# A hybrid attention encoder on one core: attention A's heads in one written sequence, branch B's results stored by token, and the first tiles scaled straight from PSUM

## The chip, the core and the metric

One core of a Trainium2 chip runs the kernel alone. Its engines have instruction queues of their own and wait for each other by semaphores: PE (TensorE, matrix products into PSUM banks), PEld (its weight loads), DVE (VectorE), ACT (ScalarE), POOL (GpSimd) and SP (SyncE, which here only issues DMA transfers). The metric is the device time of one execution in microseconds; the figure compared is the median of several runs.

## The reference

An encoder layer in float32 over 1280 tokens of 1024 channels: a sample sequence of 1024 and a prompt of 256, each attended within itself. Cut to what matters here:

```
h = rmsnorm(x, g_mix);  z = h @ w_in      # q, k, v of both branches, and two gates
o_a = banded(qa, ka, va, window 128, bias, sink)          # 8 heads, 2 kv heads
for (window, dil) in ((128, 1), (512, 4), (2048, 16)):    # 3 groups of 4 heads
    outs, lses += banded(residues(q, dil), residues(k, dil), residues(v, dil), ...)
alpha = softmax(stack(lses), axis=0);  o_b = sum(alpha * stack(outs))
merged = gate0 * (o_a @ w_branch_a) + gate1 * (o_b @ w_branch_b)
x = x + merged @ w_out
y = rmsnorm(x + relu(rmsnorm(x, g_mlp) @ w_up)**2 @ w_down, g_final)
```

`banded` is softmax attention over a query's own block of keys and the two beside it, with a table of relative biases.

## The kernel before

The tokens are ten tiles of 128 (eight of the sample, `t` 0 to 7, two of the prompt, 8 and 9). Every operand of a large product is split into a high and a low part (`hhi`, `hlo`; ACT makes the high part, DVE the rest), and a product is three matmuls: hi·lo, lo·hi, hi·hi.

**Start.** The weights of the first norm come as one row (`gm_row`); two matmuls with a row of ones (L802) spread it over the partitions into two PSUM banks, and DVE copies each half into `gm` (L803). `square(t)` sums a tile's squares on ACT and takes the root, `scale(t)` multiplies tile, reciprocal root and `gm` on DVE (L707, L708), 16 transposes on PE turn the first two tiles (L340), ACT and DVE split them (L734, L736), and the matmuls of v begin (L764) when ACT has split the first weights `vhi` (L184).

**Projections and branch B** follow in one long part with an order written by hand (`manual_schedule`). Beside its products run, as generators of small steps, branch B's attention (`att_b`), which stores each tile's result to DRAM (`scr_b`, one tensor per group; rows of 132 numbers: the outputs of two heads, their maxima and sums), and `entering()`, which prepares the next part: a raw weight load (`fetch`), queries, keys and values of the first heads (`load_unit(0)`), the biases, and half of h (`h21`, 2 MB), which had been put away in `scr_h`.

**Attention A** (from L1041). 40 steps: four units `u` of two heads, ten tiles each. A step is `scores` (four matmuls into `sc` banks, L1068 and L1069; DVE adds the bias and takes maxima, L1070 and L1074; ACT the exponentials, L1076), then `transposes` (4 or 6 on PE, L1091, copied out of the `pt` banks by DVE and ACT in turn through `copy`, L266 and L268), then `values_of` (the value matmuls, L1106, the copy of `o` and its store by POOL). The three belong to steps i, i − 1 and i − 2 of one pass. Two generators fill in: `logits()`, the gates' products (L191; blocks 0, 2 and 1 of 512, 256 and 512 tokens for each chunk of 128 columns; block 1 needs `h21`), and `merges_of`, which brings branch B's rows back (`load_rows`, six or eight DMAs on SP for two tiles) and merges the three groups by their log sums (DVE, L1158 to L1178). Up to step 36 the tile scheduler may reorder what each engine does; from there the written order holds.

**After it**: `turn_merged` and `turn_a` transpose both results, then come the branch products, gates, `w_out`, the MLP and the last norm.

Of the kernel before, what the change touches and what calls it, by code (L numbers as in the profile page):

```python
# [96 lines left out]
def encoder_kernel(  # L97
# [89 lines left out]
    def mm3(ps, pairs):  # L187

        seq = [x for (lh, ll), (rh, rl) in pairs for x in ((ll, rh), (lh, rl), (lh, rh))]
        for i, (a, b) in enumerate(seq):  # L190
            nc.tensor.matmul(ps, a, b, start=i == 0, stop=i == len(seq) - 1)  # L191
            if i % 8 == 7:
                yield
# [45 lines left out]
    def weight(ahead=None):  # L239
# [4 lines left out]
        while len(raws) < min(len(PLAIN), len(ready) + 1):  # L244
            fetch()
# [28 lines left out]
    scr_b = [dram.tile([T, 2, ROW], F32, name=f"scr_b{g}_") for g in range(3)]  # L274
# [218 lines left out]
    def attention_b(make):  # L493
# [134 lines left out]
    def entering():  # L628
# [33 lines left out]
    with ExitStack() as pre:  # L662
# [137 lines left out]
        for h in range(2):  # L800
            ps = bank("mm", "g")
            nc.tensor.matmul(ps, ones, gm_row[:, 512 * h : 512 * h + 512], start=True, stop=True)  # L802
            nc.vector.tensor_copy(gm[:, 512 * h : 512 * h + 512], ps)  # L803
        square(0)
        scale(0)
        next(turns[0])
        square(1)
        scale(1)
# [6 lines left out]
        split_v(0, 2)  # L815
        scale(2)
# [62 lines left out]
    if True:  # L879
# [159 lines left out]
        flush(True)  # L1039
    first_part.close()  # L1040
# [4 lines left out]
    if True:  # L1045
# [13 lines left out]
        def scores(u, t):  # L1059
# [4 lines left out]
            nm, l = nm_a[:, 2 * u : 2 * u + 2, t], l_a[:, 2 * u : 2 * u + 2, t]  # L1064
# [9 lines left out]
            nc.vector.scalar_tensor_tensor(nm, m, -1.0, nsink[:, 2 * u : 2 * u + 2], op0=ALU.mult, op1=ALU.min)  # L1074
            for h in range(2):
# [3 lines left out]
            live[u, t] = s  # L1079

        def transposes(u, t):
# [14 lines left out]
        def values_of(u, t):  # L1096
            lo, W, _ = tiles[t]
            pt = live.pop((u, t))
            v, rest = units[u][0]["v"]
            pv = bank("pv")  # L1100
            for h in range(2):
                for b in range(W // P):
                    k = lo + b
                    src = v[:, k, HALVES[u // 2]] if k < 8 else rest[:, k - 8, HALVES[u // 2]]
                    for rows_ in HALVES:
                        nc.tensor.matmul(pv[rows_, HD * h : HD * h + HD], pt[:, 2 * b + h, rows_], src,  # L1106
                                         start=b == 0, stop=b == W // P - 1)
# [12 lines left out]
        def logits():  # L1120

            for c in PLAIN:
                hi, lo = weight()
                for t0, n in BLOCKS[::2] + BLOCKS[1:2]:
                    ps = bank("mm")
                    yield from mm3(ps[:, :n], [((hi[:, k, :], lo[:, k, :]), h_at(k, t0, n)) for k in range(KC)])
                    z = wslot("gs", (P, 512))
                    copy(z[:, :n], ps[:, :n])
                    nc.sync.dma_start(scr_g[c][:, t0 : t0 + n], z[:, :n])

        def load_rows(i, t):
# [3 lines left out]
            r = rows_b[i, t] = wslot("r", (P, 2, 3, ROW))  # L1135
            for j in range(2):
                if t < 8:
                    a = P // 8 * (t + j)
                    nc.sync.dma_start(r[:, j, 0, :], scr_b[0][P * (t + j) : P * (t + j + 1), i, :].rearrange(
                        "(q m) c -> m q c", m=8))  # L1140
                    rows = scr_b[1][:NS, i, :].rearrange("(r q m) c -> m r q c", r=4, m=2)[:, :, a : a + 16]
                    for m in range(2):
                        nc.sync.dma_start(r[64 * m : 64 * m + 64, j, 1, :], rows[m])
                    nc.sync.dma_start(r[:, j, 2, :], scr_b[2][:NS, i, :].rearrange(
                        "(r q) c -> r q c", r=8)[:, a : a + 16])
                    continue
                nc.sync.dma_start(r[:, j, 0, :], scr_b[0][P * (t + j) : P * (t + j + 1), i, :].rearrange(
                    "(q m) c -> m q c", m=2))
                for g in (1, 2):
                    nc.sync.dma_start(r[:, j, g, :], scr_b[g][NS:, i, :].rearrange(  # L1150
                        "(r q) c -> r q c", r=2)[:, 64 * j : 64 * j + 64])

        def merge(i, t):

            r = rows_b.pop((i, t))
# [4 lines left out]
            e = small.tile([P, 2, 3, 2], F32, name="e", tag="e", bufs=2)  # L1160
# [747 lines left out]
```

## Time and profile before

| | us |
|---|---|
| median of 3 runs | 1709.33 (1706.9 to 1710.93) |
| the profiled execution, its own time | 1707.63 |
| its span in the profile | 1705.7 |
| attention A, first gate matmul of the stage to the first branch products | about 541 to 711 |

A row of a timeline is: start and duration in us, engine, line of the kernel, operation, out<-in by the program's names, shapes, count, and in brackets how long the engine sat idle before and what ended that. A row of waits is: engine, its operation and line, what it waited for; us in all, times, longest. A row of windows is: the stretch, its length, then for PE, PEld, DVE, ACT and POOL the busy time and in brackets the instructions, then the granted TensorE clock (1.00 is full), the busy share of the DMA engines and GB/s. A row of groups ends with busy us and mean ns of one, then the idle time ahead of the group and what ended it. A row of the chain is start, length and what. Matmuls are pipelined: the distance of two starts is what one costs, its printed duration is longer.

### The profile page before, as it was taken

The numbers are of one execution on the slowest core, as the hardware profiler recorded it, in microseconds if no ns is written. First come the engines' busy times: TensorE is split into PE (matmuls) and PEld (weight loads), VectorE is DVE, ScalarE is ACT, GpSimd is POOL, SyncE is SP. The second block draws the span as 40 slices with busy tenths as digits, with TensorE's granted clock in tenths as the row PEclk, the third lists the DMA queues.
The fourth block names the chain that finished last, engine by engine and source line by source line (L and its number), as shares of the span: only waits on it lengthen the run. The fifth ranks groups of instructions, "written<-read, shape, count | busy, mean of one in ns | idle before, by whom it ended". The sixth has DMA issues, their size and how long they took to land.

```text
span 1705.7 us, 26610 instructions
## 1 busy us (share of the span) xinstructions
PE 1687.7 (99%) x9956; PEld 1428.6 (84%) x9956; DVE 987.7 (58%) x1712; ACT 720.2 (42%) x1538; POOL 422.7 (25%) x384
## 2 busy tenths in 40 slices
PE   8999999999999999999999999999999999999998
PEld 7898888888888887888888888888888888888886
DVE  7634553554441676576568545454546767667565
ACT  7232544444442455554266433433334433333345
POOL 0211122121111111000100255464555332314150
PEclk9999999999999999999999999999999999999999
DMA  6315566564536663466012434433447844633333
GB/s 234 117 62 124 161 176 196 174 193 131 152 116 188 189 168 94 167 209 243 26 75 75 137 116 148 157 117 120 158 134 251 299 142 150 213 113 118 117 118 124
DMA packets 234604, 255.84 MB, mean 150 GB/s; under 512 B 30433, under 2 KB 164661, under 8 KB 234347
## 3 DMA queue, kind: packets, MB, share of 16 engines
q1 hardware_dynamic: 225752, 231.27, 42.9%
q0 software_dynamic: 7344, 20.24, 3.7%
q10 hardware_dynamic: 1378, 2.63, 0.4%
q8 instruction: 79, 1.29, 0.3%
q14 instruction: 51, 0.41, 0.1%
HBM read 168.58 MB, written 90.73 MB: 152 GB/s over the span
## 4 chain that ended last, share of the span: by engine, by line
PE 94%; DMA 2%; DVE 2%; SPq 1%; issue 1%; ACT 1%; DVEq 0%; ACTq 0%
PE dn L351 21%; PE x L351 19%; PE mm L191 14%; PE z L351 9%; PE v L764 6%; PE pv L351 5%; PE y L351 5%; PE mm L351 5%; PE pv L1106 2%; PE sc L543 1%; PE pt L1091 1%; PE pv L589 1%; PE tr L340 1%; PE pt L568 1%; PE sc L1068 1%
## 5 line engine op out<-in xcount | busy, mean ns | idle before, releaser
L351 PE MATMUL dn<-dhi,ulo 128*128 128x512 f32 x448 | 173.9, 390 | 0.7 <-DVE ulo L185 0.7
L351 PE MATMUL dn<-dhi,uhi 128*128 128x512 f32 x448 | 173.9, 389 | 0.0
L351 PE MATMUL dn<-dlo,uhi 128*128 128x512 f32 x448 | 173.9, 389 | 0.0
L351 PE MATMUL x<-chi,wlo 128*128 128x512 f32 x424 | 166.8, 393 | 0.0
L351 PE MATMUL x<-clo,whi 128*128 128x512 f32 x424 | 165.7, 391 | 0.0
L351 PE MATMUL x<-chi,whi 128*128 128x512 f32 x424 | 165.2, 390 | 0.0
L316 DVE TENSOR_TENSOR wlo<-ta,whi 128x1024 fp32r<-128x1024 f32 x30 | 55.2, 1840 | 161.0 <-ACT whi L314 161.0
L316 DVE TENSOR_TENSOR wlo<-raw,whi 128x1024 fp32r<-128x1024 f32 x60 | 88.6, 1477 | 88.8 <-ACT whi L314 88.8
L385 POOL TENSOR_TENSOR tb<-raw 128x512 f32<-128x512 f32 x16 | 20.8, 1301 | 346.6 <-DMA raw<-in_w_up_dram 205.5
L351 PEld LDWEIGHTS dn<-dhi,ulo 128*128 128x128 f32 x448 | 84.1, 188 | 18.7 <-DVE ulo L185 1.2
L351 PEld LDWEIGHTS dn<-dlo,uhi 128*128 128x128 f32 x448 | 84.1, 188 | 17.4
L351 PEld LDWEIGHTS dn<-dhi,uhi 128*128 128x128 f32 x448 | 84.0, 188 | 17.3
L351 PEld LDWEIGHTS x<-chi,wlo 128*128 128x128 f32 x424 | 79.8, 188 | 17.2 <-issue 1.8
L351 PEld LDWEIGHTS x<-chi,whi 128*128 128x128 f32 x424 | 79.6, 188 | 16.9
L185 DVE TENSOR_TENSOR ulo<-uraw,uhi 128x1024 fp32r<-128x1024 f32 x56 | 86.1, 1557 | 10.9 <-ACT uhi L184 10.9
L351 PEld LDWEIGHTS x<-clo,whi 128*128 128x128 f32 x424 | 79.8, 188 | 15.1 <-DVE clo L316 0.4
L1590 POOL TENSOR_TENSOR t<-raw,t 128x1024 f32<-128x1024 f32 x16 | 46.6, 2930 | 146.6 <-DMA raw<-in_w_down_dram 142.3
L1746 DVE TENSOR_TENSOR v<-v,dn 128x512 f32<-128x512 f32 x90 | 59.4, 681 | 40.0 <-PE dn L351 37.2
L351 PE MATMUL dn<-dhi,up 128*128 128x512 f32 x224 | 73.5, 389 | 0.0
L553 DVE CUSTOM_DVE_ANT_0 s<-sc,bias 128x128 f32<-128x128 f32 (+1 forms) x120 | 36.3, 340 | 64.3 <-PE sc L543 64.3
L351 PE MATMUL z<-chi,wlo 128*128 128x512 f32 x184 | 72.0, 391 | 0.0
L351 PE MATMUL z<-chi,whi 128*128 128x512 f32 x184 | 71.7, 390 | 0.0
(350 smaller groups left out, 4640.6 us busy)
## 6 DMA issues: line engine op xcount, KB each, us to landing
scr_u<-u SPq DMA_DIRECT2D x112, 320.0 KB
uraw<-scr_u SPq DMA_DIRECT2D x56, 512.0 KB
raw<-in_w_in_dram SPq DMA_DIRECT2D x33, 512.0 KB
raw<-in_w_up_dram SPq DMA_DIRECT2D x32, 512.0 KB
raw<-in_w_down_dram SPq DMA_DIRECT2D x28, 512.0 KB
sg<-scr_g SPq DMA_DIRECT2D x32, 256.0 KB
uraw<-scr_u SPq DMA_DIRECT2D x28, 256.0 KB
v<-scr_v SPq DMA_DIRECT2D x96, 64.0 KB
```

The source lines that it names most:

```text
L185: nc.vector.tensor_tensor(lo, src, hi.bitcast(F32), op=ALU.subtract)
L191: nc.tensor.matmul(ps, a, b, start=i == 0, stop=i == len(seq) - 1)
L316: nc.vector.tensor_tensor(lo, src, hi.bitcast(F32), op=ALU.subtract)
L340: nc.tensor.transpose(ps[:, P * i : P * (i + 1)], xn[t][:, P * k : P * (k + 1)], ident)
L351: nc.tensor.matmul(ps, a, b, start=first and i == 0, stop=last and i == len(seq) - 1, skip_group_check=True)
L385: eng.tensor_tensor(tb[:, 0], b12, b11, op=ALU.subtract)
L543: nc.tensor.matmul(ps[p0 : p0 + nq, c : c + W], qk[d, b, q : q + nq], qk[d, b, k : k + W], start=True, stop=True)
L553: nc.vector.tensor_tensor_reduce(d, src, bt, 1.0, -3.0e38, op0=ALU.add, op1=ALU.max, accum_out=m[:, h : h + 1])
L764: nc.tensor.matmul(ps[:, :n], a, b, start=k == 0 and j == 0, stop=k == KC - 1 and j == 2)
L1106: nc.tensor.matmul(pv[rows_, HD * h : HD * h + HD], pt[:, 2 * b + h, rows_], src, start=b == 0, stop=b == W // P - 1)
L1590: (eng or nc.gpsimd).tensor_tensor(o, a, b, op=ALU.subtract)
L1746: nc.vector.tensor_tensor(v, v, ps, op=ALU.add)
```

## The change

Four parts.

1. **Start.** `scale_first` scales the first two tiles from the PSUM banks of the spread weights, in halves of 512 columns; the copies into `gm` come ahead of the third tile's scale. Ten transposes of the identity into a bank that nobody reads stand around the spreading matmuls (four ahead, six behind).
2. **Entry of attention A.** The reloads of `h21` move from `entering()` behind the last pair of projections; two more raw weight loads are issued ahead of them. The gates' blocks are taken in another order: blocks 0 and 2 of two chunks first, and 18 fill steps of four matmuls of 512 (or eight of 256) precede the first scores.
3. **Attention A.** All 40 steps are in written order, in pairs: in each half of a pair scores, transposes of the step two before, merge steps, exponentials, one fill step; once a pair the values of two steps into one bank, copied out by one DVE instruction. All copies out of `pt` go to ACT.
4. **Branch B by token.** `scr_b` is one tensor with a token's three groups side by side. `att_b` stores to strided tokens; `load_rows` is one DMA; the merge's sums are a generator of their own (`alpha_steps`). The gate logits go to `scr_g` by POOL's queue, no longer by SP's.

DVE at the program's start, after the two constants: `gm` is the norm's weights in SBUF, `g` the PSUM banks of the spread. Before, then now:

```order
L803 COPY gm<-g 128x512 x2
L707 RECIPROCAL rs<-sd 128x1
L708 SCALAR_TENSOR_TENSOR xn<-xt,rs,gm 128x1024
L707 RECIPROCAL rs<-sd 128x1
L708 SCALAR_TENSOR_TENSOR xn<-xt,rs,gm 128x1024
L736 TENSOR_TENSOR hlo<-tr,hhi 128x2x128 x4
```

```order
L815 RECIPROCAL rs<-sd 128x1
L819 SCALAR_TENSOR_TENSOR xn<-xt,rs,g 128x512 x2
L815 RECIPROCAL rs<-sd 128x1
L819 SCALAR_TENSOR_TENSOR xn<-xt,rs,g 128x512 x2
L739 TENSOR_TENSOR hlo<-tr,hhi 128x2x128 x4
L185 TENSOR_TENSOR vlo<-vraw,vhi 128x1024
L739 TENSOR_TENSOR hlo<-tr,hhi 128x2x128 x4
L185 TENSOR_TENSOR vlo<-vraw,vhi 128x1024 x2
L834 COPY gm<-g 128x512 x2
```

The two copies left the head of the queue and stand behind three splits of v's weights.

SP's queue where the projections end (`scr_g<-z` are the last pair's stores, `hhi` and `hlo` from `scr_h` the reloads of `h21`, `raw` a weight load). Before, then now:

```order
L434 DMA va<-scr_v 128x8x128
L893 DMA scr_g_136<-z 128x512
L639 DMA hhi<-scr_h_143 128x1024
L639 DMA hlo<-scr_h_143 128x1024
L639 DMA hhi<-scr_h_144 128x1024
L639 DMA hlo<-scr_h_144 128x1024
L893 DMA scr_g_137<-z 128x512
L893 DMA scr_g_137<-z 128x256
L221 DMA raw<-in_w_in_dram 128x8x128
```

```order
L434 DMA va<-scr_v 128x8x128
L912 DMA scr_g_134<-z 128x512
L912 DMA scr_g_135<-z 128x512
L912 DMA scr_g_135<-z 128x256
L221 DMA raw<-in_w_in_dram 128x8x128
L1063 DMA hhi<-scr_h_141 128x1024
L1063 DMA hlo<-scr_h_141 128x1024
L1063 DMA hhi<-scr_h_142 128x1024
L1063 DMA hlo<-scr_h_142 128x1024
```

The reloads moved behind two more stores and one weight load.

PE in the middle of attention A (`mm` gate products, `sc` scores, `pt` transposes, `pv` values). Before, then now:

```order
L191 MATMUL mm<-hlo,whi 128x512
L1106 MATMUL pv<-va,pt 64x64 x9
L1091 MATMUL pt<-ident,s 128x128 x2
L1106 MATMUL pv<-va,pt 64x64 x3
L1068 MATMUL sc<-kk,q 128x384
L1091 MATMUL pt<-ident,s 128x128 x4
L1069 MATMUL sc<-kk,q 128x384
L191 MATMUL mm<-hhi,whi 128x512
L1068 MATMUL sc<-kk,q 128x384
```

```order
L1092 MATMUL sc<-kk,q 128x384
L1093 MATMUL sc<-kk,q 128x384
L1092 MATMUL sc<-kk,q 128x384
L1093 MATMUL sc<-kk,q 128x384
L1136 MATMUL pv<-va,pt 64x64 x24
L1119 MATMUL pt<-ident,s 128x128 x6
L191 MATMUL mm<-hlo,whi 128x512
L191 MATMUL mm<-hhi,whi 128x512
L191 MATMUL mm<-hhi,wlo 128x512
L191 MATMUL mm<-hlo,whi 128x512
L1092 MATMUL sc<-kk,q 128x384
```

The values of two steps stand in one group (the trace has two records for each of these matmuls), and nothing comes between them.

The diff, cut to its core:

```diff
-    def mm3(ps, pairs):
+    def mm3(ps, pairs, few=4):
...
-            if i % 8 == 7:
+            if i % few == few - 1:
                 yield
...
-        while len(raws) < min(len(PLAIN), len(ready) + 1):
+        while len(raws) < min(len(PLAIN), len(ready) + 2):
             fetch()
...
-    scr_b = [dram.tile([T, 2, ROW], F32, name=f"scr_b{g}_") for g in range(3)]
+    scr_b = dram.tile([T, 2, 3, ROW], F32, name="scr_b")
...
-                        nc.gpsimd.dma_start(scr_b[g][qa : qa + nq, i, :], o[p0 : p0 + nq, c + x, :])
...
+                        nc.gpsimd.dma_start(scr_b[first : first + step * (nq - 1) + 1 : step, i, g, :],
+                                            o[p0 : p0 + nq, c + x, :])
...
     def entering():
         fetch()
         yield
+        bias0 = load_bias(0, wslot)
         yield
-        unit0 = load_unit(0), load_bias(0, wslot)
+        fetch()
+        unit0 = load_unit(0), bias0
         yield
-        for i in range(2):
-            h21[i] = slot("hhi", (P, 2, 512), F32R), slot("hlo", (P, 2, 512), F32R)
-            for j in range(2):
-                nc.sync.dma_start(h21[i][j].bitcast(F32), scr_h[i][:, j])
         prepare()
...
-        for h in range(2):
-            ps = bank("mm", "g")
-            nc.tensor.matmul(ps, ones, gm_row[:, 512 * h : 512 * h + 512], start=True, stop=True)
-            nc.vector.tensor_copy(gm[:, 512 * h : 512 * h + 512], ps)
+        idle = bank("sc", "idle")
+        spread_gm = []
+        for h in range(3):
+            for _ in range((4, 0, 6)[h]):
+                nc.tensor.transpose(idle[:, :P], ident, ident)
+            if h < 2:
+                ps = bank(("mm", "pv")[h], "g")
+                nc.tensor.matmul(ps, ones, gm_row[:, 512 * h : 512 * h + 512], start=True, stop=True)
+                spread_gm.append(ps)
+        def scale_first(t):
...
+            for h in range(2):
+                c = slice(512 * h, 512 * h + 512)
+                nc.vector.scalar_tensor_tensor(xn[t][:, c], x[:, c], rs, spread_gm[h], op0=ALU.mult, op1=ALU.mult)
...
         split_v(0, 2)
+        for h in range(2):
+            nc.vector.tensor_copy(gm[:, 512 * h : 512 * h + 512], spread_gm[h])
         scale(2)
...
     flush(True)
+    fetch()
+    for i in range(2):
+        h21[i] = slot("hhi", (P, 2, 512), F32R), slot("hlo", (P, 2, 512), F32R)
+        for j in range(2):
+            nc.sync.dma_start(h21[i][j].bitcast(F32), scr_h[i][:, j])
...
-                copy(pt[:, i:e, :], ps[:, : P * (e - i)].rearrange("p (i q) -> p i q", q=P))
+                nc.scalar.activation(pt[:, i:e, :], ps[:, : P * (e - i)].rearrange("p (i q) -> p i q", q=P), AF.Copy)
...
-            o = a3("o", (P, P), 4)
-            copy(o, pv[:, :P])
-            nc.gpsimd.dma_start(scr_o[t][:, P * u : P * u + P], o)
+            o = a3("o", (P, 2, P), 3)
+            nc.vector.tensor_copy(o, pv[:, : 2 * P].rearrange("p (x c) -> p x c", c=P))
+            for x, (u, t) in enumerate(steps):
+                nc.gpsimd.dma_start(scr_o[t][:, P * u : P * u + P], o[:, x, :])
...
+            first, last = PLAIN[0], PLAIN[-1]
+            seq = [(first, 0), (first, 2), (first + 1, 0), (first + 1, 2), (first, 1), (first + 1, 1)]
+            seq += [(c, b) for c in PLAIN[2:] for b in (0, 2, 1)]
...
-                    nc.sync.dma_start(scr_g[c][:, t0 : t0 + n], z[:, :n])
+                nc.gpsimd.dma_start(scr_g[c][:, t0 : t0 + n], z[:, :n])
...
-            r = rows_b[i, t] = wslot("r", (P, 2, 3, ROW))
...
+            r = rows_b[i, t] = slot("r", (P, 2, 3, ROW))
+            nc.sync.dma_start(r.rearrange("p j g c -> p j (g c)"),
+                              scr_b[P * t : P * t + 2 * P, i].rearrange("(j p) g c -> p j (g c)", p=P))
...
             for n, x in enumerate(seq):
+                now = merge(*x)
+                next(now)
+                coming = alpha_steps(*seq[n + 1]) if n + 1 < len(seq) else iter(())
+                next(coming, None)
                 yield
...
+                if n + 2 < len(seq):
+                    load_rows(*seq[n + 2])
+                next(now)
+                yield
+                next(coming, None)
+                yield
...
+        def merge_steps(i, j):
+            while done[1] < 50 * (i + j - 1) / 35:
+                next(merges, None)
+                done[1] += 1
...
-        steps_of(fill, 6)
-        for i in range(len(order) + 2):
-            if i == 36:
-                ctx.enter_context(tc.manual_schedule(engines=ALL))
...
+        ctx.enter_context(tc.manual_schedule(engines=ALL))
+        steps_of(fill, 18)
+        for i in range(0, len(order) + 4, 2):
+            for j in range(2):
...
+                    scores(u, t)
+                    if j == 0 and i > 2:
+                        values_of(*order[i - 4 : i - 2])
...
+                if 0 < i < len(order) + 2:
+                    transposes(*order[i + j - 2])
+                merge_steps(i, j)
+                if i < len(order):
+                    exponentials(*order[i + j])
+                steps_of(fill, 2 if i > len(order) - 2 or j and i > 30 else 1)
...
-            next(fill)
+            steps_of(fill, 2)
```

More of the change, by code (lines that the diff above doesn't have):

```diff
@@ L1074, in scores, with exponentials @@
             nc.vector.scalar_tensor_tensor(nm, m, -1.0, nsink[:, 2 * u : 2 * u + 2], op0=ALU.mult, op1=ALU.min)
+            live[u, t] = s
+        def exponentials(u, t):
+            s, W = live[u, t], tiles[t][1]
+            nm, l = nm_a[:, 2 * u : 2 * u + 2, t], l_a[:, 2 * u : 2 * u + 2, t]
             for h in range(2):
@@ L1092, in transposes, with values_of @@
             for i, e, ps in banks:
-                copy(pt[:, i:e, :], ps[:, : P * (e - i)].rearrange("p (i q) -> p i q", q=P))
+                nc.scalar.activation(pt[:, i:e, :], ps[:, : P * (e - i)].rearrange("p (i q) -> p i q", q=P), AF.Copy)
             live[u, t] = pt
[L1096 to L1099, printed above, removed]
+        def values_of(*steps):
             pv = bank("pv")
[L1101 to L1107, printed above, removed]
-            o = a3("o", (P, P), 4)
-            copy(o, pv[:, :P])
-            nc.gpsimd.dma_start(scr_o[t][:, P * u : P * u + P], o)
+            for x, (u, t) in enumerate(steps):
+                lo, W, _ = tiles[t]
+                pt = live.pop((u, t))
+                v, rest = units[u][0]["v"]
+                for h in range(2):
+                    c = P * x + HD * h
+                    for b in range(W // P):
+                        k = lo + b
+                        src = v[:, k, HALVES[u // 2]] if k < 8 else rest[:, k - 8, HALVES[u // 2]]
+                        for r in HALVES:
+                            nc.tensor.matmul(pv[r, c : c + HD], pt[:, 2 * b + h, r], src,
+                                             start=b == 0, stop=b == W // P - 1)
+            o = a3("o", (P, 2, P), 3)
+            nc.vector.tensor_copy(o, pv[:, : 2 * P].rearrange("p (x c) -> p x c", c=P))
+            for x, (u, t) in enumerate(steps):
+                nc.gpsimd.dma_start(scr_o[t][:, P * u : P * u + P], o[:, x, :])
         def sums_a():
@@ L1120, in logits @@
         def logits():
[L1122 to L1128, printed above, removed]
-                    nc.sync.dma_start(scr_g[c][:, t0 : t0 + n], z[:, :n])
-        def load_rows(i, t):
-            r = rows_b[i, t] = wslot("r", (P, 2, 3, ROW))
[L1136 to L1151, printed above, removed]
@@ L1153, in merge @@
-        def merge(i, t):
-            r = rows_b.pop((i, t))
+            first, last = PLAIN[0], PLAIN[-1]
+            seq = [(first, 0), (first, 2), (first + 1, 0), (first + 1, 2), (first, 1), (first + 1, 1)]
+            seq += [(c, b) for c in PLAIN[2:] for b in (0, 2, 1)]
+            ws, coming = {}, iter(())
+            for c, b in seq:
+                if c not in ws:
+                    ws[c] = weight(0)
+                    coming = prepare_steps()
+                    next(coming)
+                (hi, lo), (t0, n) = ws[c], BLOCKS[b]
+                ps = bank("mm")
+                yield from mm3(ps[:, :n], [((hi[:, k, :], lo[:, k, :]), h_at(k, t0, n)) for k in range(KC)],
+                               2048 // n)
+                z = wslot("gs", (P, 512))
+                copy(z[:, :n], ps[:, :n])
+                nc.gpsimd.dma_start(scr_g[c][:, t0 : t0 + n], z[:, :n])
+                next(coming, None)
@@ L1169, in merge @@
             yield
+        def merge(i, t):
+            r, e = rows_b.pop((i, t)), alphas.pop((i, t))
             for j in range(2):
@@ L1182, in merges_of @@
             load_rows(*seq[0])
+            yield
+            load_rows(*seq[1])
+            for _ in range(4):
+                yield
+            coming = alpha_steps(*seq[0])
+            next(coming)
+            yield
+            yield
+            next(coming)
+            yield
             for n, x in enumerate(seq):
+                now = merge(*x)
+                next(now)
+                coming = alpha_steps(*seq[n + 1]) if n + 1 < len(seq) else iter(())
+                next(coming, None)
                 yield
-                if n + 1 < len(seq):
-                    load_rows(*seq[n + 1])
-                yield from merge(*x)
+                next(now)
+                yield
+                if n + 2 < len(seq):
+                    load_rows(*seq[n + 2])
+                next(now)
+                yield
+                next(coming, None)
+                yield
         rows_b = {}
@@ L1348, in encoder_kernel @@
                 open_gate(i)
-            next(fill)
+            steps_of(fill, 2)
         run(fill)
```

76 lines of the change are left out of this document (33 added, 43 removed).

## The prediction

> **What bounds the kernel now.** I read the page's busy times first, then what TensorE waited for, and then the stage of attention A, which most of the change touches.
>
> ```profile
> span 1705.7 us, 26610 instructions
> PE 1687.7 (99%) x9956; PEld 1428.6 (84%) x9956; DVE 987.7 (58%) x1712; ACT 720.2 (42%) x1538; POOL 422.7 (25%) x384
> ...
> PE tr L340 <- DVE rs L707: 2.3, 1, 2.3
> PE mm L191 <- DMA hhi<-scr_h: 2.1, 1, 2.1
> PE pt L1091 <- ACT s L1076: 1.1, 2, 0.8
> ...
> 541.00:711.40 170.40, 165.95 (x1571) 137.21 (x1570) 102.26 (x400) 83.00 (x249) 23.75 (x43) 0.98 0.55 155
> ```
>
> TensorE bounds it everywhere: only 18 us of the span is idle on it, and DVE (102.3 of 170.4 us) and ACT (83.0) have room in attention A (541 to 711.4). So the change can gain in three ways only: by the few waits named here (2.3 at the start, 2.1 and 1.1 in attention A, and what belongs to them), by clock lost behind them, and by time that looks busy, where matmuls of different kinds follow each other slowly. I price the three in turn.
>
> **The start.**
>
> ```profile
> 0.74 0.52 ACTq L775 DMA_DIRECT2D row<-in_g_mix_dram  x1
> ...
> 2.29 3.75 PE L802 MATMUL g<-row,ones 1*128 1x512 f32 x4 [2.29 <-DMA row<-in_g_mix_dram]
> ...
> 5.75 0.29 ACT L703 ACTIVATE sd<-ss,eps 128x1 f32<-128x1 f32 x1
> ...
> 6.08 0.69 DVE L803 COPY gm<-g 128x512 f32<-128x512 f32 x1 [1.02 <-PE g L802]
> ...
> 6.88 1.29 DVE L708 SCALAR_TENSOR_TENSOR xn<-xt,rs,gm 128x1024 f32<-128x1024 f32 x1
> ...
> 8.31 3.64 PE L340 MATMUL tr<-ident,xn 128*128 128x128 f32 x16 [2.27 <-DVE rs L707]
> ...
> 10.83 1.06 ACT L184 ACTIVATE vhi<-vraw 128x1024 fp32r<-128x1024 f32 x1
> ...
> 11.94 1.86 PE L764 MATMUL v<-vhi,hhi 128*128 128x512 f32 x4
> ...
> 13.63 1.09 PE L764 MATMUL v<-vlo,hhi 128*128 128x512 f32 x4
> ```
>
> The second copy of the norm's weights starts at 6.08 and delays the first scale to 6.88, although the standard deviation is there at 6.04. Without the copies the reciprocal runs at 6.1, the first half of the scale (half of 1.29) from 6.3 to 6.95, and the transposes, which now wait for halves, can start at about 7.1 instead of 8.31: 1.2 us earlier. All 16 of them took 3.64 us, 0.23 each; the first matmul waits for vhi's split on ACT, which is behind the hhi copies of those transposes and moves with them. The ten idle transposes at 0.23 each fill 0.9 us ahead of the g matmuls, while those wait for their row (2.29), and 1.4 us behind them, from 6.04: done by 7.4, so at worst 0.3 us late. The two copies (1.38 us of DVE) come back ahead of the third tile's scale, where the matmuls of v are already fed four at a time; some of the gain can be lost there. I take **−1.2**, between −0.3 (copies collide with vlo) and −2.2 (the transposes also run fast: the first four v matmuls took 1.86 us against 1.09 for the next four, and 16 transposes at half their time would be 1.8 us shorter, less what the vhi chain on ACT holds back).
>
> The Trainium skill, "TensorE: Matmul & The Clock Gate", Part 4 (on transposes in PE mode), says that the clock gate does not engage for transposes, which speaks against the idle ones. The trace agrees as far as it goes: sixteen transposes from 8.31 left the first v matmuls slow. By that rule the start gives −1.2 and not more, as taken here.
>
> **The wait for the h reloads.** Before, the third block of the stage's first weight chunk reads the half of h that is loaded back from DRAM, and those loads are not there.
>
> ```profile
> 549.58 0.28 PE L1068 MATMUL sc<-kk,q 128*128 128x256 f32 x1
> 549.70 0.28 PE L1069 MATMUL sc<-kk,q 128*128 128x256 f32 x1
> 552.12 0.47 PE L191 MATMUL mm<-hhi,wlo 128*128 128x512 f32 x1 [2.14 <-DMA hhi<-scr_h]
> 553.15 0.79 PE L191 MATMUL mm<-hlo,whi 128*128 128x512 f32 x1 [0.56 <-DMA hlo<-scr_h]
> 553.74 0.63 PE L191 MATMUL mm<-hhi,whi 128*128 128x512 f32 x1
> 554.17 0.63 PE L191 MATMUL mm<-hhi,wlo 128*128 128x512 f32 x1
> ...
> 556.23 0.40 PE L191 MATMUL mm<-hhi,whi 128*128 128x512 f32 x1
> 556.46 0.40 PE L191 MATMUL mm<-hhi,wlo 128*128 128x512 f32 x1
> ...
> 553.70:556.20 2.50, 2.50 (x7) 1.80 (x6) 0.00 (x0) 0.00 (x0) 0.00 (x0) 0.52 1.11 359
> ```
>
> From 549.70 to 556.23 the TensorE did one score and nine matmuls; at 0.12 and 0.23 each (the first two rows stand 0.12 apart, the last two matmuls 0.23) that is 2.2 us of work in 6.5: the hole is worth 4.4 (idle, and then matmuls 0.43 apart, as at 553.74, at a granted clock of 0.52). Now 18 fill steps stand ahead of the first pair of tiles: two chunks' blocks of 512 and of 256, 24 matmuls each, so 48 × 0.23 + 48 × 0.12 = 17 us from 541, and the reloaded block is needed at about 558.5. Its loads are issued later, behind the last stores of z, and two more weight loads of 512 KB stand ahead of them. At the 359 GB/s of the last row that 1 MB costs 3 us: they land near 555 to 557. **−4.4**, with 1.5 to 3 us to spare; if it is missed, up to the 4.4 come back.
>
> The Trainium skill, same page, "Why this matters for your kernels", tells to keep TensorE gaps under about 3 us for the clock to stay up. Here a gap of 2.14 and one of 0.56 already cost it. By that rule the hole would be worth its idle time alone.
>
> **The wait for branch B's rows.**
>
> ```profile
> 665.62 0.16 DVE L1158 TENSOR_TENSOR mm__7404<-r 128x4 f32<-128x4 f32 x1 [1.88 <-DMA r<-scr_b__83]
> ...
> 666.71 0.33 PE L1091 MATMUL pt<-ident,s 128*128 128x128 f32 x1 [0.81 <-ACT s L1076]
> ...
> 667.31 0.55 PE L1091 MATMUL pt<-ident,s 128*128 128x128 f32 x3 [0.27 <-ACT s L1076]
> 667.50 0.16 DVE L1159 TENSOR_TENSOR mm__7404<-mm__7404,r 128x4 f32<-128x4 f32 x1 [1.64 <-DMA r<-scr_b__84]
> ...
> 668.52 0.50 PE L1091 MATMUL pt<-ident,s 128*128 128x128 f32 x2 [0.67 <-DVE pt L268]
> ...
> 668.80:672.20 3.40, 3.40 (x27) 3.06 (x26) 3.22 (x15) 1.69 (x5) 0.30 (x1) 0.50 0.14 42
> ...
> 659.76 7.61 DMA r<-scr_b__84
> ```
>
> DVE stands for two of a merge's six loads, one after the other; the maxima of the next scores stand behind them on DVE, and TensorE waits 0.81 + 0.27 + 0.67 for exponentials and copies. It then runs 3.4 us at a clock of 0.50, half of it lost: 1.75 + 1.7, and with some 0.5 (an estimate) for the matmuls between the waits, which are slow too, **4.0**. The last of the six loads, which SP issues one after the other, takes 7.61 us from issue to landing (the chain's row). Now one load of 256 rows of 1584 bytes does it. Two bounds for its latency: 1.55 us for a short load (in_g_mix's issue at 0.74, matmul at 2.29) plus 405 KB at 359 GB/s (1.1) gives 2.7; the row above gives 7.6. It is issued in the third of a merge's four steps and used two steps later at the nearest; 50 steps are spread over 35 halves of a pair of tiles, at 3.2 us a half (below), so 4.4 us, and TensorE feels a delay only some 1.8 us after DVE does (1.88 + 1.64 on DVE against 1.75 on PE). So it may take about 6 us. I take 3 to 4 with a weight load ahead of it, nearer to the short row: **−4.0**.
>
> **The order in attention A.**
>
> ```profile
> 640.94 0.60 PE L1091 MATMUL pt<-ident,s 128*128 128x128 f32 x4
> 641.47 0.92 PE L1106 MATMUL pv<-va,pt 128*64 128x64 f32 x24
> 642.32 0.50 PE L191 MATMUL mm<-hhi,whi 128*128 128x512 f32 x1
> 642.65 0.33 PE L1068 MATMUL sc<-kk,q 128*128 128x384 f32 x1
> 642.83 0.34 PE L1069 MATMUL sc<-kk,q 128*128 128x384 f32 x1
> ...
> 644.25 0.44 PE L1106 MATMUL pv<-va,pt 128*64 128x64 f32 x6
> ...
> 645.21 0.80 PE L1106 MATMUL pv<-va,pt 128*64 128x64 f32 x18
> ...
> L1091 PE MATMUL pt<-ident,s 128*128 128x128 f32 x208 | 34.7, 278 | 1.7 <-ACT s L1076 1.1 <-DVE pt L268 0.7
> ...
> L268 DVE COPY pt<-pt 128x512 f32<-128x512 f32 (+1 forms) x33 | 19.7, 597 | 14.6 <-PE pt L1091 14.5
> ```
>
> A change of kind into and out of the value matmuls is slow. Inside a group they stand 0.03 apart (18 last 0.36 longer than 6). From 641.47 to 642.65 are 1.18 us; less 24 × 0.03 and one fill matmul of 0.23 that is 0.23, and ahead of it 641.47 − 640.94 less four transposes at 0.11 ((0.60 − 0.28) / 3, one being 0.28 long) another 0.09: about 0.3 for a group, 0.2 where transposes follow. Before, the stage has 55 such groups: 40 steps, some cut by the scheduler, as the 24 into 6 and 18 here. Now one group holds two steps and nothing cuts it: 20 groups. The number of matmuls, transposes and scores stays. 35 × 0.28 = **−10** (−7 at 0.2; −12 at 0.32).
>
> Is there a new bound? A pair of tiles costs PE 8 scores at 0.18 (the two score rows), 48 values at 0.03, 12 transposes at 0.11, 8 fill matmuls at 0.23 and one change: 6.3 us. ACT, busy 83.0 us in the stage, takes over DVE's 19.7 us of copies of transposed tiles: 103 us at most, 5.1 for each of 20 pairs. That leaves 1.2 us a pair, and the exponentials have two halves of 3.2 us until their transposes. DVE, at 102 of 170 us, loses those copies. So ACT stays under PE, but not by much.
>
> The gate logits' stores go from SP to POOL, busy for 24 of the stage's 170 us; there they stand behind the stores of o, which wait for DVE's copies, and only the copy into the same buffer some blocks later waits for them: nothing. Branch B's results are written in the same pieces of 528 bytes, only at other addresses: nothing, between 0 and +1.5. The tail of the stage (o loads together, two fill steps a turn) reorders the same work: 0 ± 1.5.
>
> **Sum**: −1.2 − 4.4 − 4.0 − 10 = −19.6. The profiled execution took 1707.6 (span 1705.7 and 1.9 around it), so 1688.0; the median of the runs lies 1.7 above that execution, and I put the new median at **1689**.
>
> **Rivals.**
> - One of the two holes stays (the reloads past 558.5, or a row load over 6 us once): +4 to +4.4, 1693. Against it stand margins of 2 us; for it, DMA shares of 1.11 at that place. 0.18.
> - A group change costs by the kinds, not by the count, so that fewer groups save nothing: 1699. Against: the 0.3 was read at single groups. 0.07.
> - The clock only falls after about 3 us, so the holes are worth their idle time (2.7 + 1.75 instead of 8.4): 1693. The two rows at 0.52 and 0.50 speak against it. 0.02.
> - ACT becomes the bound: if its 5.1 us a pair grow to 7.1, 0.8 past PE's (copies waiting for banks in strict order), 20 pairs give back 16 us: 1705, within 0.2%. 0.04.
> - **Slower**: the row loads come late. If the one load takes the 7.6 us of the chain's row, seven of the ten merges (three are loaded ahead) stall as the one above did, at 4.0: +28, 1717. It decides from a latency of about 6 us. Against: one load instead of six in a row on SP. 0.05.
>
> My forecast has 0.64. The range 1682 to 1701 goes from −2.2 at the start, −12 and −1.5 of the tail below to the rival without gain from groups above. A measurement of this kernel tells 0.2% (3.4 us) from no change: faster 0.91, same 0.04, slower 0.05.
>
> **What would show it.** First v matmul at 10.4 to 11; no TensorE wait on hhi, hlo or on s near a merge, and no window of the stage below a clock of 0.9; the stage about 152 us instead of 170.4 with values in 20 groups of up to 48; DVE waits on r under 2 us. I am wrong if the stage lies over 160, or if the stages behind it (1705.7 − 711.4 = 994 us) move by more than 2.

## The result and the profile after

| | before | after |
|---|---|---|
| median of the runs, us | 1708.12 (1706.61 to 1710.93, 4 runs) | 1687.39 (1686.09 to 1687.96, 4 runs) |
| profiled execution / its span | 1707.63 / 1705.7 | 1687.32 / 1685.5 |
| first matmul of v | 11.94 | 11.16 |
| first matmul of the projections (L351) | 116.68 | 115.62 |
| first gate matmul of attention A's stage | 541.00 | 540.50 |
| the stage, up to the first transpose of o | 170.35 | 150.82 |

The kernel before has one run more here than ahead of the prediction, so that its median is 1708.12 and no longer 1709.33. The ratio is 0.9876, 95% interval 0.9859 to 0.9893: 20.7 us faster, against 20 forecast. The span is 20.2 shorter, 19.5 of it in attention A's stage (18.4 forecast). The page's head, the longest of TensorE's waits, and the stage as one window, each of the changed kernel:

```profile
span 1685.5 us, 26457 instructions
PE 1673.6 (99%) x9966; PEld 1424.6 (85%) x9966; DVE 980.9 (58%) x1682; ACT 727.3 (43%) x1550; POOL 429.3 (25%) x399
```

```profile
PE idle L807 <- POOL ident masks.py:199: 1.5, 1, 1.5
PE sc L1092 <- DVE m L1094: 0.8, 2, 0.5
PE dn L351 <- DVE ulo L185: 0.7, 1, 0.7
PE mm L191 <- DMA hlo<-scr_h: 0.6, 2, 0.3
```

```profile
540.50:691.30 150.80, 149.38 (x1570) 131.35 (x1569) 96.65 (x369) 91.66 (x262) 31.16 (x57) 1.00 0.63 185
```

No wait in the stage is over 0.5 us (the first row belongs to the start, `dn` to the MLP), and the granted clock is 1.00 over all of it (0.98 before). ACT went from 83.0 to 91.7 us of work while the stage shrank, and still has 59 us to spare.

The start in the timeline of the changed kernel:

```profile
2.51 3.78 PE L810 MATMUL g<-row,ones 1*128 1x512 f32 x4
...
6.12 1.40 DVE L819 SCALAR_TENSOR_TENSOR xn<-xt,rs,g 128x512 f32<-128x512 f32 x2
6.22 1.54 PE L807 MATMUL idle<-ident 128*128 128x128 f32 x6
...
7.55 3.62 PE L340 MATMUL tr<-ident,xn 128*128 128x128 f32 x16
...
11.16 1.68 PE L767 MATMUL v<-vhi,hhi 128*128 128x512 f32 x4
...
12.68 1.07 PE L767 MATMUL v<-vlo,hhi 128*128 128x512 f32 x4
```

The first half tile is scaled at about 6.8 (half of 1.40 from 6.12), but the transposes begin at 7.55 with no wait in brackets: the six idle ones, from 6.22, held the queue.

The entry of attention A, and one pair of its tiles, in the same timeline:

```profile
546.24 4.10 SPq L1063 DMA_DIRECT2D hhi<-scr_h  x1
...
558.35 0.50 PE L191 MATMUL mm<-hlo,whi 128*128 128x512 f32 x1 [0.30 <-DMA hlo<-scr_h]
...
561.75 0.50 PE L191 MATMUL mm<-hlo,whi 128*128 128x512 f32 x1 [0.29 <-DMA hlo<-scr_h]
...
595.64 0.34 PE L1093 MATMUL sc<-kk,q 128*128 128x384 f32 x1
595.91 1.39 PE L1136 MATMUL pv<-va,pt 128*64 128x64 f32 x40
597.23 0.88 PE L1119 MATMUL pt<-ident,s 128*128 128x128 f32 x6
597.86 0.48 PE L191 MATMUL mm<-hhi,whi 128*128 128x512 f32 x1
```

The reloads of h came just late: two waits of 0.3, with the clock at 1.00 behind them, instead of waits of 2.14 and 0.56 and a clock of 0.52. The values of a tile of 256 keys and one of 384 now stand in one unbroken group of 40 records.

### The profile page after: what moved, and what is told of

Read it like the earlier page. It is cut to its first block, busy times and chain, and to the rows that moved or that the text cites. A ratio compares the mean times of both kernels' runs of the same rounds, so it can differ in the third digit from the quotient of the medians.

```text
span 1685.5 us, 26457 instructions
## 1 busy us (share of the span) xinstructions
PE 1673.6 (99%) x9966; PEld 1424.6 (85%) x9966; DVE 980.9 (58%) x1682; ACT 727.3 (43%) x1550; POOL 429.3 (25%) x399
## 4 chain that ended last, share of the span: by engine, by line
PE 93%; DMA 3%; DVE 2%; ACT 1%; issue 1%; SPq 0%; POOL 0%; DVEq 0%; ACTq 0%; POOLq 0%
PE dn L351 21%; PE x L351 18%; PE mm L191 14%; PE z L351 9%; PE v L767 6%; PE pv L351 5%; PE y L351 5%; PE mm L351 4%; PE pv L1136 2%; PE pt L1119 1%; PE sc L543 1%; PE pv L589 1%; PE tr L340 1%; PE pt L568 1%; DMA v<-scr_v 1%; DMA scr_qa<-z 1%
## 5 line engine op out<-in xcount | busy, mean ns | idle before, releaser
L351 PE MATMUL dn<-dhi,ulo 128*128 128x512 f32 x448 | 173.7, 389 | 0.7 <-DVE ulo L185 0.7
L351 PE MATMUL dn<-dhi,uhi 128*128 128x512 f32 x448 | 173.8, 389 | 0.0
L351 PE MATMUL dn<-dlo,uhi 128*128 128x512 f32 x448 | 173.8, 389 | 0.0
L351 PE MATMUL x<-chi,wlo 128*128 128x512 f32 x424 | 166.7, 393 | 0.0
L351 PE MATMUL x<-clo,whi 128*128 128x512 f32 x424 | 165.6, 391 | 0.0
L351 PE MATMUL x<-chi,whi 128*128 128x512 f32 x424 | 165.1, 389 | 0.0
L609 POOL DMA_DIRECT2D scr_b<-o x72 | 39.0, 545 | 257.2 <-ACT o L600 202.0
L351 PEld LDWEIGHTS dn<-dhi,ulo 128*128 128x128 f32 x448 | 84.1, 188 | 18.7 <-DVE ulo L185 1.1
L351 PEld LDWEIGHTS dn<-dlo,uhi 128*128 128x128 f32 x448 | 84.1, 188 | 17.3
L351 PEld LDWEIGHTS dn<-dhi,uhi 128*128 128x128 f32 x448 | 84.0, 188 | 17.4
L351 PEld LDWEIGHTS x<-chi,wlo 128*128 128x128 f32 x424 | 79.8, 188 | 17.2 <-issue 1.8
L351 PEld LDWEIGHTS x<-chi,whi 128*128 128x128 f32 x424 | 79.6, 188 | 16.9
L351 PEld LDWEIGHTS x<-clo,whi 128*128 128x128 f32 x424 | 79.8, 188 | 15.1 <-DVE clo L316 0.4
L351 PE MATMUL dn<-dhi,up 128*128 128x512 f32 x224 | 73.5, 389 | 0.0
L351 PE MATMUL z<-chi,wlo 128*128 128x512 f32 x184 | 71.9, 391 | 0.0
```

Of the source, the lines that this page charges most:

```text
L351: nc.tensor.matmul(ps, a, b, start=first and i == 0, stop=last and i == len(seq) - 1, skip_group_check=True)
L609: nc.gpsimd.dma_start(scr_b[first : first + step * (nq - 1) + 1 : step, i, g, :], o[p0 : p0 + nq, c + x, :])
```

## The experiments

The distances below are read where the part in question ends: at the first projection matmul for the start, over the stage for the rest. Between the two, branch B's waits move the start of the stage by up to a microsecond from run to run (539.4 to 540.6 in most runs of the changed kernel and its variants with the same start, once 543.9), so a whole time says less than these.

**The groups of value matmuls.** One step instead of two in a group (e1), and each head of a step by itself (e2):

```diff
-                    if j == 0 and i > 2:
-                        values_of(*order[i - 4 : i - 2])
+                    if i > 2:
+                        values_of(order[i + j - 4])
```

> The changed kernel with the values of one step at a time: 40 groups of value matmuls instead of 20, each copied out by its own DVE instruction; all else as changed. Theory (each group costs about 0.21 us where transposes follow it): 20 more groups, stage of attention A 150.8 -> about 155, time +4. Rival (a change of kind costs nothing by the count): within 0.5 us of the changed kernel.

```diff
-                    scores(u, t)
-                    if j == 0 and i > 2:
-                        values_of(*order[i - 4 : i - 2])
+                    if i > 2:
+                        values_half(*order[i + j - 4], 0)
+                    scores(u, t)
+                    if i > 2:
+                        values_half(*order[i + j - 4], 1)
```

> The changed kernel with the values of one step cut in two: one head ahead of the scores, the other behind them, so 80 groups. Theory: 20 groups more that end in transposes (0.21 each) and 40 more between fill matmuls and scores (0.32 each): +17, stage about 168, still with no hole in it. Rival: within 1 us of the changed kernel.

The stage of e1 as one window, then that of e2:

```profile
543.90:699.76 155.86, 154.87 (x1570) 132.26 (x1569) 98.63 (x389) 91.88 (x262) 31.30 (x57) 1.00 0.62 182
```

```profile
540.63:709.30 168.67, 167.27 (x1571) 133.53 (x1569) 97.83 (x389) 92.14 (x262) 31.31 (x57) 1.00 0.58 168
```

The same PE records (within one), the same clock of 1.00, hardly more or less idle time (1.0 and 1.4 us, 1.4 in the changed kernel), and 155.9 and 168.7 us instead of 150.8: +5.05 for 20 groups more (0.25 each), +17.85 for 56 more (0.32 each; the last four steps have no scores between their halves, so that the trace has 76 groups, not 80). The medians are 1692.97 (1692.30 to 1696.69) and 1704.91 (1703.78 to 1707.26). With 76 groups the kernel is almost back where it was (ratio to before 0.9982, interval 0.9972 to 0.9991). That groups cost by their number is shown; the rival is out.

**The order of the gate blocks** (e3):

```diff
-            seq = [(first, 0), (first, 2), (first + 1, 0), (first + 1, 2), (first, 1), (first + 1, 1)]
-            seq += [(c, b) for c in PLAIN[2:] for b in (0, 2, 1)]
+            seq = [(c, b) for c in PLAIN for b in (0, 2, 1)]
```

> The changed kernel with the gate products' blocks in the old order (0, 2, 1 of each chunk), so that the reloaded half of h is needed after 9 fill steps, 8.3 us into the stage, instead of after 18. Theory: the first hlo lands at about 558 as in the changed kernel, so TensorE waits some 9 us there and then runs about 3 us at half clock: +10 to +11. Rival (other work of the stage was what was late, not these loads): +1 or less.

Its timeline at the hole, and a window behind it:

```profile
556.05 0.77 PE L191 MATMUL mm<-hhi,wlo 128*128 128x512 f32 x1 [7.72 <-DMA hhi<-scr_h]
557.57 0.80 PE L191 MATMUL mm<-hlo,whi 128*128 128x512 f32 x1 [0.75 <-DMA hlo<-scr_h]
558.16 0.63 PE L191 MATMUL mm<-hhi,whi 128*128 128x512 f32 x1
558.59 0.63 PE L191 MATMUL mm<-hhi,wlo 128*128 128x512 f32 x1
```

```profile
555.00:560.00 5.00, 3.20 (x7) 2.07 (x7) 0.00 (x0) 0.00 (x0) 0.00 (x0) 0.50 1.07 335
```

The stage takes 161.09, +10.3, as forecast: 8.5 idle, and matmuls 0.43 apart at a clock of 0.50 behind it. The time is 1697.39 (1696.33 to 1701.02). So the order of blocks is what keeps TensorE off the reloads.

**Where the reloads are issued** (e7): back in `entering()`, blocks in the new order.

```diff
         unit0 = load_unit(0), bias0
         yield
+        for i in range(2):
+            h21[i] = slot("hhi", (P, 2, 512), F32R), slot("hlo", (P, 2, 512), F32R)
+            for j in range(2):
+                nc.sync.dma_start(h21[i][j].bitcast(F32), scr_h[i][:, j])
```

> The changed kernel with the four reloads of h issued where they were before the change, in the entry to attention A, ahead of the last stores; the blocks stay in the new order. Theory (the order of the blocks alone removes the hole; moving the loads back costs the two short waits on hlo, 0.3 each, with 0.15 more around each): the two waits go, stage 150.8 -> 149.9. Rival (the early loads take the DMA engines from the last pair's weights or from queries and keys): a new wait of 1 us or more ahead of or in the stage.

What its engines waited for between 538 and 575:

```profile
...
DVE wlo L233 <- ACT whi L231: 17.6, 2, 12.5
ACT whi L231 <- DMA raw<-in_w_in_dram: 14.1, 1, 14.1
...
PE sc L1092 <- DVE m L1094: 4.8, 1, 4.8
```

A miss: the stage takes 155.99 instead of 149.9, and the time is 1692.03 (1690.02 to 1693.86). Both waits on hlo are gone, but the third weight chunk now stands behind 2 MB of reloads. ACT waits for it until 560.09 (until 555.54 in the changed kernel), DVE waits for ACT's half of the split, and the maxima of the first scores stand behind that split on DVE, so the second scores find no free bank: TensorE waits 4.8 and then runs at a clock of 0.50 up to 567.2. That is a new wait in the stage, as the rival had it, though it took another road. Putting the reloads last lets the weights through first; that is worth 5 us, which the prediction did not see at all.

**Branch B's rows**: the layout alone on the kernel before (e4; its diff is the change's for `scr_b`, the store, `load_rows` and `turn_merged`, with the loads issued where they were), and six loads on the changed kernel (e8):

```diff
-            nc.sync.dma_start(r.rearrange("p j g c -> p j (g c)"),
-                              scr_b[P * t : P * t + 2 * P, i].rearrange("(j p) g c -> p j (g c)", p=P))
+            for j in range(2):
+                for g in range(3):
+                    nc.sync.dma_start(r[:, j, g, :], scr_b[P * (t + j) : P * (t + j + 1), i, g, :])
```

> The kernel before with the layout of branch B's results alone changed: one tensor by token, one load of two tiles instead of six or eight, issued as early as before. Theory (one load lands in about 4 us, the wait on branch B's rows and the half clock behind it go): -4, time about 1704. Rival (what counts is that the changed kernel issues the loads a merge earlier): the waits for r on DVE stay, time within 1 us of before.

> The changed kernel with each load of branch B's rows cut into six (128 rows of 528 bytes each), issued at the same place, a merge ahead. Theory (one load removes the wait): six issues hold SP some 3 to 10 us and the last lands as late as before, DVE waits on r by 1 to 3 us at several merges, +3 to +10. Rival (the lead of a merge removes the wait, however many loads): DVE waits stay under 1 us and the time within 1.5 us of the changed kernel.

The transfers of the rows in the changed kernel, in e4 and in e8 (KB each, median us from issue to landing), and in e8 DVE's two longest waits for them:

```profile
r<-scr_b SPq DMA_DIRECT2D x10, 396.0 KB, 3.8
```

```profile
r<-scr_b SPq DMA_DIRECT2D x10, 396.0 KB, 4.5
```

```profile
r<-scr_b SPq DMA_DIRECT2D x60, 66.0 KB, 2.4
```

```profile
DVE mm__6429 L1187 <- DMA r<-scr_b: 2.7, 1, 2.7
DVE mm__6020 L1187 <- DMA r<-scr_b: 2.1, 1, 2.1
```

e4 takes 1702.28 (1701.57 to 1703.24; ratio to before 0.9964, 0.9951 to 0.9976), 5.5 less, and its stage 165.33 instead of 170.35; DVE no longer waits for a row anywhere. What those 5.0 us consist of, the windows tell: the stage of e4 and its stretch at a lowered clock, then the two such stretches of the kernel before.

```profile
540.92:706.25 165.33, 162.43 (x1570) 136.54 (x1569) 103.37 (x400) 83.11 (x249) 23.86 (x43) 0.98 0.55 160
```

```profile
551.87:558.70 6.83, 5.89 (x13) 4.19 (x14) 0.94 (x5) 0.13 (x1) 0.00 (x0) 0.50 0.89 290
```

```profile
552.71:556.12 3.41, 2.97 (x7) 2.23 (x8) 0.00 (x0) 0.00 (x0) 0.00 (x0) 0.50 1.07 370
668.76:672.17 3.41, 3.41 (x27) 3.07 (x26) 3.23 (x15) 1.69 (x5) 0.34 (x1) 0.50 0.14 43
```

TensorE's idle time falls from 4.4 to 2.9 us, since the three waits behind the rows (1.75) are gone. The time at half clock does not fall: the hole at the reloads, still there with waits of 2.48 and 0.42, now has 6.83 us at 0.50 behind it, as much as both holes had before. Most of the other 3.5 us lies in the scheduler's order, which came out otherwise with other instructions: 49 groups of values instead of 55 (1.5 to 1.9 us at 0.25 to 0.32), 55 of transposes instead of 64, 51 of scores instead of 63. So e4 shows that the layout alone removes the waits; it does not show that it saves the clock behind them. The start-alone kernel e9, whose attention A is that of before, adds to the doubt. Its rows come as late, and its clock does not fall behind them:

```profile
668.01 0.33 PE L1107 MATMUL pt<-ident,s 128*128 128x128 f32 x1 [0.89 <-ACT s L1092]
668.61 0.55 PE L1107 MATMUL pt<-ident,s 128*128 128x128 f32 x3 [0.27 <-ACT s L1092]
669.93 0.44 PE L1107 MATMUL pt<-ident,s 128*128 128x128 f32 x2 [0.78 <-DVE pt L268]
```

```profile
551.97:558.80 6.83, 6.42 (x14) 4.55 (x15) 0.94 (x5) 0.73 (x3) 0.00 (x0) 0.50 0.90 284
668.00:674.00 6.00, 4.88 (x50) 3.83 (x52) 5.00 (x19) 2.92 (x10) 0.91 (x2) 1.00 0.42 158
```

Waits of this size were once followed by half clock and once not.

In e8 the waits on r come back (2.7 and 2.1 us), though its loads have the longer lead, and the stage takes 152.5, the median 1689.85 (1688.41 to 1695.57; the changed kernel 1687.39): +1.7 in the stage, less than forecast, because TensorE feels only part of what DVE waits. The single load does it, with either lead; with six the lead alone is not enough for DVE, and almost enough for TensorE.

**The start.** The new start alone on the kernel before (e9), and the changed kernel without the idle transposes (e5, as in the diff) or with only the four ahead (e6, which has 4, 0, 0 there):

```diff
-            for _ in range((4, 0, 6)[h]):
+            for _ in range((0, 0, 0)[h]):
```

> The kernel before with the new start alone (first two tiles scaled from PSUM, copies of the norm's weights later, ten idle transposes). Theory (the parts add): first v matmul at 11.2, first projection matmul at 115.6 instead of 116.7, attention A as before with both holes, time -1. Rival (the earlier start is given back at the third tile, where the copies now stand): first projection matmul at 116.4 or later.

> The changed kernel without the ten idle transposes. Theory (they keep no clock up and only hold the queue: the first half tile is scaled at 6.8, the real transposes start at 7.55 behind them): transposes from about 7.0, first v matmul at 10.6 instead of 11.16, first projection matmul at 115.1 instead of 115.6. Rival (they open the clock earlier): first four v matmuls slower than the 1.68 us of the changed kernel, and the first projection matmul later than 115.6.

> The changed kernel with the four idle transposes ahead of the spreading matmuls and without the six behind them. Theory: as without any, first v matmul at about 10.6, since the four run while the norm's row is still on its way. Rival (they open the clock): earlier than without any.

The timeline of e5:

```profile
6.15 1.40 DVE L818 SCALAR_TENSOR_TENSOR xn<-xt,rs,g 128x512 f32<-128x512 f32 x2
...
7.04 3.30 PE L340 MATMUL tr<-ident,xn 128*128 128x128 f32 x16 [1.04 <-DVE xn L818]
...
10.68 1.21 PE L767 MATMUL v<-vhi,hhi 128*128 128x512 f32 x4 [0.33 <-ACT vhi L184]
...
11.94 1.19 PE L767 MATMUL v<-vlo,hhi 128*128 128x512 f32 x4
```

Without the idle transposes the real ones start half a microsecond earlier, and the first projection matmul comes at 115.01 (e5) and 114.98 (e6) instead of 115.62. All profiled kernels with the new start agree: 115.42 to 115.62 in the eight that have the six idle transposes behind the spread, 114.98 to 115.12 in the three that do not (e11 below is the third). So the six cost 0.3 to 0.6 us.

The pace of the first v matmuls, which e5's expectation named as the sign, tells nothing about them. With all ten idle transposes, the changed kernel run once more (e10, below) and e1; without any, e11:

```profile
11.17 1.20 PE L767 MATMUL v<-vhi,hhi 128*128 128x512 f32 x4
```

```profile
7.55 2.68 PE L340 MATMUL tr<-ident,xn 128*128 128x128 f32 x16
```

```profile
10.65 1.66 PE L767 MATMUL v<-vhi,hhi 128*128 128x512 f32 x4
```

With the ten, the first four v matmuls took 1.19 to 1.68; without the six, 1.21 to 1.66. In each run TensorE's pace doubles at some moment of the start. In e1 it is at 9.2, amid the sixteen transposes, which stand 0.21 apart ahead of it and 0.11 behind; in the changed kernel it is at about 12.2. Over the eight runs with the ten it lies between 9.1 and 12.2, over the three others between 9.8 and 11.7. Whether the idle ones bring it forward is therefore left open by these runs. (The granted clock in the windows reads 1.00 all through the start, so that only the distances tell.)

The single times of e5 and e6 were 1686.06 and 1687.07. In e9 that matmul comes at 115.49, 1.2 earlier than before; by the start of the stage (540.84 against 541.00) waits in branch B had taken it back in that run, and its time, 1708.44 beside 1709.12 for before, can't be told from it.

**What the written order adds** (e12): the kernel before with the rows by token and with the new entry and block order, but the old start and the scheduler's layout of attention A. It also lacks what came with the written order: the copies out of `pt` by ACT alone, the merge's sums as a generator, the gate stores on POOL's queue.

```diff
-        steps_of(fill, 6)
+        steps_of(fill, 12)
...
-            while done[0] * 120 < 31 * n and done[0] < 31:
+            while done[0] * 120 < 25 * n and done[0] < 25:
```

> The kernel before with branch B's rows by token and with the new entry and order of blocks, but with attention A still laid out by the scheduler (46 groups of value matmuls) and the old start. Theory (both holes go, and what is left to the changed kernel's 150.8 is the 26 groups more, at 0.25 to 0.32 each): stage 157 to 159, no TensorE wait on hhi, hlo or s over 0.5, time about 1697. Rival (the written order gains more than the groups, by waits that the scheduler's order brings): stage 162 or more, with such waits in it.

Its waits of TensorE, a window at a lowered clock, and its whole stage:

```profile
PE pt L1099 <- ACT s L1084: 2.8, 2, 2.5
...
PE mm L191 <- DVE wlo L233: 1.4, 1, 1.4
PE mm L191 <- DMA hlo<-scr_h: 1.1, 1, 1.1
```

```profile
572.00:574.00 2.00, 2.00 (x9) 1.90 (x8) 1.14 (x6) 0.60 (x1) 0.00 (x0) 0.50 1.01 258
541.49:705.99 164.50, 160.46 (x1570) 135.83 (x1569) 106.17 (x399) 83.04 (x249) 23.77 (x43) 0.99 0.56 159
```

The rival held: the stage takes 164.5, the time is 1702.76 (1701.23 to 1705.01), no better than e4 without the new entry. The old holes are gone but for 1.1 us on hlo, and a new one opened: TensorE waits 2.5 for exponentials, up to 568.59, and stands at a clock of 0.50 a few microseconds later. Of the 13.7 us between it and the changed kernel, 2.6 are idle time (4.0 against 1.4) and 1.7 the half of a stretch of 3.4 us at half clock (570.8 to 574.2). The other 9.4 lie in the order: the 26 groups above the changed kernel's 20 make 6.5 to 8.3 of them, and the scheduler also left 53 groups of transposes and 45 of scores, where the changed kernel has 40 of each. In this form the new entry gains nothing without the written order and what came with it.

**A version without what the runs found wanting** (e11), beside the changed kernel (e10): no idle transposes, and the half-reloaded block summed from the kept half first.

```diff
-                yield from mm3(ps[:, :n], [((hi[:, k, :], lo[:, k, :]), h_at(k, t0, n)) for k in range(KC)],
+                yield from mm3(ps[:, :n], [((hi[:, k, :], lo[:, k, :]), h_at(k, t0, n))
+                                          for k in ((4, 5, 6, 7, 0, 1, 2, 3) if b == 1 else range(KC))],
                                2048 // n)
```

> The changed kernel once more, as the measure for the next one: 1687.4 within 0.5, stage of attention A 150.8 within 0.5; its start of the stage differs by up to 1 us from run to run with branch B's waits.

> The changed kernel without the idle transposes, and with the block of h that is half reloaded summed from the half that was kept (channels 512 to 1023 first), so that the reloads are needed 12 matmuls = 2.7 us later. Theory: -0.6 at the start as in the run without idle transposes, and both waits on hlo go (0.3 each with some 0.15 around each): -0.9, in all -1.5, 1685.9. Rival (the scores wait for the same time then, since DVE and DMA set the pace there): the waits on hlo become waits of sc on DVE, -0.6 alone.

e10 gave 1689.30 (1687.06 to 1690.73; ratio to before 0.989, 0.9874 to 0.9907), a median 1.9 above the first one, so the expectation of 0.5 was too narrow; its stage took 151.13. e11 gave 1686.76 (1685.34 to 1687.70; ratio 0.9872, 0.9857 to 0.9887). Its first projection matmul comes at 115.12 against 115.53, and its stage takes 150.42. Its waits on hlo are gone, and 1.4 us of waits of sc on DVE (0.6 in e10) stand in their place, as the rival had it. The intervals overlap: better by a microsecond or two is likely, but not shown.

## Why the prediction was right

The change gained in the three ways named, and the time lies at the forecast. The sum fits better than its terms: in attention A the holes gave less than forecast and the order more, and that the two errors nearly cancel is luck.

- **Bound and ways to gain.** Right: TensorE is busy 99% before and after, and the stages behind attention A moved by 0.1 us.
- **Start, −1.2.** Measured −1.06 at the first projection matmul (−1.2 in e9), inside −0.3 to −2.2. The old start itself varies (116.27 in e4, 116.68, 117.29 in e12), so that −0.7 to −1.9 would have been measured by other pairs of runs. The step on the idle transposes was mis-sized: they were to be done by 7.4 and cost at most 0.3. They began at 6.22, ended near 7.6, and the six cost 0.3 to 0.6. The Trainium skill, "TensorE: Matmul & The Clock Gate", Part 4, has it that the gate does not engage for transposes. The runs do not bear this out: in e1 and e9 the pace doubles amid the transposes, about 2 us ahead of the first v matmul. The slow v matmuls that the prediction took as agreement are one case of a moment that moves from run to run.
- **Reloads, −4.4.** The mechanism was right, the margin wrong: 1.5 to 3 us to spare were forecast, and the first hlo was 0.3 late (558.35). Before, the hole was worth 4.2: 2.7 idle, and half of the 2.97 us of work at half clock. What was missed is the path of the third weight chunk: the order of the loads mattered by 5 us (e7), and not for the reloads' own sake.
- **Branch B's rows, −4.0.** The load takes 3.8 us (3 to 4 forecast), and the layout by itself removes the 1.75 of waits (e4). The 1.7 for the clock behind them was there in the run of before, but not in e9 with the same waits. For the 0.5 on slow matmuls between the waits no run shows anything: the stretch at 0.50 begins at 668.76, behind the last of the three.
- **Groups, −10.** At 0.25 to 0.32 a group (e1, e2), 35 fewer make −8.8 to −11.2. The groups of transposes and scores that the scheduler had cut as well, 64 and 63 against 40 and 40 now, were put at nothing.
- **The sum.** Of the stage's −19.5, idle time is 3.0 (4.4 to 1.4) and half clock 3.2 (half of the 6.38 us of work done in the two stretches). That is 6.2, where 8.4 was forecast for the two holes. The other 13.3 lie in the order, where 10 was forecast; the value groups explain 8.8 to 11.2 of them. What the remaining 2 to 4.5 are is not shown: the groups of transposes and scores are the likeliest, but no run varied them alone. A condition was also left unsaid: the holes go only if nothing new opens, and in the scheduler's order something did (e12).
- **Signs.** The stage (150.8 for 152), the groups, the clock, DVE's wait for rows (0.9) and the stages behind came as said. Two did not: the first v matmul came at 11.16 instead of 10.4 to 11, and TensorE waited for hlo twice, 0.3 each.
- **Rivals.** Slower by late rows: they land in 3.8 us, and DVE waited for one once, 0.9. ACT as the bound: 91.7 of 150.8 us. The clock falling only after about 3 us: waits of 2.14 (before), 2.48 (e4), 2.15 (e9) and 2.5 (e12) were each followed by a clock of 0.50, so this falls for gaps of that size. Single waits of up to 1.1 in the stage (e8) left it at 1.00; the three short waits for rows did the one in the run of before and the other in e9.
- **Small slips.** 6.5 less 2.2 is 4.3, not 4.4; 35 × 0.32 is 11.2, not 12; 1688.0 and 1.7 give 1689.7, not 1689; and the terms named for the lower end of the range give 1684.5, not 1682. None changes the forecast.

## What to carry to other kernels

Where TensorE is 99% busy, count the changes of kind in its stream: the distance of starts across a group, less the distance inside it, gives a price per group, and gathering small matmuls of two steps into one bank pays it half as often. Count every kind of group that the new order changes, not one alone. Afterwards, split the measured gain into idle time, time at a lowered clock and the rest: a sum can be right with its terms wrong. A hole that a later need removes reopens elsewhere if an in-order queue (here DVE's maxima behind a weight split, behind a load) is left out of the account: follow each load to what stands behind its consumer. Filler work placed to keep an engine's clock up is worth a run without it, and more than one: the same start gave first v matmuls of 1.19 and of 1.68 us.

## What was not expected

- The same short waits for branch B's rows were followed by half clock in the run of before and by full clock in e9, and the same hole at the reloads by 3.4 us of half clock in the one and 6.8 in the other. What a hole costs in clock is not a property of the hole alone.
- Issuing 2 MB of reloads earlier made the kernel 4.6 us slower (e7, 1692.03 against 1687.39), since a 512 KB weight load then stood behind them.
- The changed kernel, run a second time, gave medians 1.9 us apart (1687.39 and 1689.30), while its stage differed by 0.3 (150.82 and 151.13); one profiled run of e1 began its stage 3.4 us later than the changed kernel did, with a wait of 2.3 us in branch B.
